# A planned TensorE order for the gate and pooling projections of a hybrid decoder block

## The chip, the cores and the metric

The kernel runs on one core of a Trainium2 chip, as one program. The metric is device time in microseconds (us); lower is better. Three runs of the kernel before gave 1358.35 to 1358.66, median 1358.63. A profiled execution of its own took 1358.44, and its trace is what is read below.

## The reference, cut to what matters

One layer of a decoder trunk steps 288 tokens (256 of a prompt, 8 samples of 4 tokens) of width 2048. All arrays are float32.

```
mod = silu(c) @ w_ada + b_ada                 # 9 conditionings x (6 parts x 2048)
h   = rmsnorm(x)*norm1 * (1 + sc1) + sh1      # parts 0, 1
u_pool, z, xbc, dt = split(h @ w_in)          # 512, 1536, 2560, 24 columns
pool_out = grouped causal means of u_pool, minus u_pool, @ pool_w[g] * pool_scale
xbc = silu(causal_conv4(xbc));  dt = softplus(dt + dt_bias)
y   = ssd_scan(xbc, dt) + D*x                 # 4 groups of 6 heads of 64, state 128
y   = rmsnorm(y * silu(z)) * ssd_norm
x   = x + g1 * (concat(pool_out, y) @ w_out)  # part 2
h2  = rmsnorm(x)*norm2 * (1 + sc2) + sh2      # parts 3, 4
x   = x + g2 * conv_ffn(h2)                   # part 5
```

## The kernel before, in words

Features lie on the partitions and tokens in the free dimension, so a projection is a series of matmuls with a 128x128 weight tile and 288 moving columns. For float32 accuracy each weight tile is split into a high and a low part of type fp32r (`split`, line 290: a ScalarE cast at line 286, a VectorE subtraction at line 288), the activations likewise, and each product is three fp32r matmuls (`mm3`, lines 300 to 302). All other TensorE work is plain float32: conditioning, transposes, the scan, the pooling maps, sums over partitions. One exception is `cse` (line 793), which is fp32r.

The stages follow one another: the first conditioning parts together with the `xbc` projections, the gate and pooling projections (`uz`, `uz_units`, line 885), the output projection (`out`), the up projections, and the down projections. This case is about `uz`: eight output tiles m = 10 to 15 (gates `z` of scan groups 2 and 3) and then m = 1 and 0 (pooling columns). `project_units` (line 306) yields every two k tiles, so one tile is 8 units of 6 matmuls, and the stage has 64 units.

Between units other generators are advanced by `pull`, each with a rate:

- `adas`: conditioning parts 2, 3 and 4 (`ada_part_units`, line 402). One visit loads four 512 KB pieces of `w_ada` and runs eight fp32 matmuls (16 rows in the trace, `adap`, line 329); the nine conditionings fill only 32 columns, so four of them lie beside each other in the array. Eight visits make a part; then come a copy (`asb`) and transposes with the bias (`adat`).
- `back`: the depthwise convolutions (`conv_group`, line 663), loads of the initial states (`h0s`), and the scan (`ssd_group`, line 714) of four groups. A scan group has transposes `xt` and `bt`, the products `cb`, state sums `s`, the old state's share `yo`, decays (`cse` on TensorE; Relu and Exp on ScalarE; products on VectorE) and, for each of three head pairs, the `y` products (lines 811 to 821), followed by line 823 and line 827 on VectorE and Square (line 829) on ScalarE.
- `y_norm` (line 896) sums the squares over partitions (`ysum`), takes sqrt on ScalarE and reciprocal on VectorE, spreads it with a matmul (`pbrstdy`) and scales the four `zy` tiles. `pool_units` (line 857) is the pooling.

The generators fix the program order only. Which instruction of an engine goes first is settled when the program is built, by the framework's scheduler, from its own estimate of when operands are ready and from priorities; on the chip each engine then runs its fixed order. `in_order` (line 208) adds dependences that hold the named engines to program order; before, it is used only at the very start.

Silu of z in groups 2 and 3 is taken straight from PSUM, tile by tile (line 893); groups 0 and 1 are taken three tiles at once (line 836). Eight raw weight buffers serve `uz` and `adap` loads in turn, all issued on SP (line 267); the state loads are issued there as well (line 702).

Of the kernel before, what the change touches and what calls it, by code (L numbers as in the profile page):

```python
# [12 lines left out]
F32 = mybir.dt.float32  # L13
# [5 lines left out]
P = 128  # L19
# [34 lines left out]
RA1, RA2, RB1, RB2, RB3 = 0.5, 0.4, 1.0, 1.0, 1.0  # L54
TA, ADA_OUT = 4, 4
TK = 4
# [105 lines left out]
def kernel(ctx: ExitStack, tc, ins, outs):  # L162
# [57 lines left out]

    wps = aux("warm")
# [104 lines left out]
    def ada_mm(ps, raw, k, c0, nb, js):  # L326
        for j in js:
            c = c0 + (j - js[0]) * nb
            nc.tensor.matmul(ps[32 * j:32 * j + 32, :nb], sc_c[:, k, :], raw[:, c:c + nb],  # L329
                             start=(k == 0), stop=(k == KT - 1), tile_position=(0, 32 * j))  # L330

# [331 lines left out]
    def conv_group(g):  # L663
# [5 lines left out]
        for r in range(5):  # L669
# [5 lines left out]
            for i in range(1, 4):  # L675
# [10 lines left out]
        nc.scalar.activation(cf[:, :, 0:NP], cf[:, :, 0:NP], AF.Silu)  # L686

        nc.scalar.activation(cf[:, :, NP:N].rearrange("p m (b l) -> p m b l", b=NB),
                             cf[:, :, 3 + NP:].rearrange("p m (b l) -> p m b l", l=7)[:, :, :, 0:NL], AF.Silu)
        yield  # L690
# [23 lines left out]
    def ssd_group(g):  # L714
# [12 lines left out]
        for c in range(3):  # L727
            pt = aux(f"xt{g}_{c}")
            for t in range(3):
                nc.tensor.transpose(pt[:, t * P:(t + 1) * P], toks(t, c), ident)  # L730
            nc.vector.tensor_tensor(heads(xdt[:, c, :]), heads(pt[:, :G6]), bc64(dt[:, c, hs]), ALU.mult)
            nc.vector.tensor_tensor(heads(xde[:, c, :]), heads(pt[:, :G6]), bc64(dtr["dtde"][:, c, hs]), ALU.mult)
# [13 lines left out]
        nc.vector.tensor_tensor(cb, pcb[:, :N], vec[:, K_TRI:K_TRI + N], ALU.mult)  # L746
# [3 lines left out]
        nc.gpsimd.dma_start(sbx[q, P:P + G6], xde[0:NS, 2, :])  # L750
        yield
# [20 lines left out]
        for i in range(2):  # L772
            for j in range(4):
# [5 lines left out]
        nc.vector.tensor_tensor(yo.rearrange("p (h q) -> p h q", h=HG),  # L779
                                py[:, :G6].rearrange("p (h q) -> p h q", h=HG),  # L780
                                bc64(dtr["ecs4"][:, hs]), ALU.mult)
        yield

        csr, cs = dtr["csr"], dtr["cs"]

        def decays(t):

            e = sx[0].tile([P, 2, N], F32, tag="e", name=f"e{g}_{t}", bufs=2)
# [630 lines left out]
```

## Time and profile before

| what | before |
|---|---|
| median of three runs | 1358.63 us |
| profiled execution, its own time | 1358.44 us |
| span of its trace | 1356.6 us |
| TensorE matmul busy | 1343.0 us |
| VectorE / ScalarE / GpSimd busy | 810.8 / 579.2 / 222.1 us |
| mean granted TensorE clock | 0.998 of 2.4 GHz |

The span is what the trace covers, from the first instruction to the last; 1.8 us of the execution lie around it. PE is TensorE, PEld its weight loads, DVE VectorE, ACT ScalarE, POOL GpSimd, SP SyncE. The record of a matmul is longer than its turn in the pipeline (matmuls of `uz` start 0.13 us apart and are recorded as 0.29 us), so starts are compared, not lengths. In the trace a plain float32 matmul leaves two rows. The page lists where the chain that ended last spent its time: 96% on PE.

### The profile page before, as it was taken

Reading aid. Unit: us, or ns where it says so; the run is one execution under the profiler, and the core shown is the slowest. Engines: PE = TensorE matmul, PEld = TensorE weight load, DVE = VectorE, ACT = ScalarE, POOL = GpSimd, SP = SyncE. Lnnn points to the kernel's source line nnn. Section 1 sums busy time; section 2 is a strip of 40 time slices with the busy share of each in tenths; the row PEclk is TensorE's granted clock in tenths of the full one; section 3 lists DMA queues with packets and bytes.
Section 4 is the critical chain, followed back from the end, with each engine's and each line's share of the span. In section 5 each row is a group of like instructions: output and inputs, shape, how many; then the busy total and the mean of one; then the engine's idle time right before and its main releaser. Section 6 shows DMA issues by size and latency. Waiting matters only on the chain.

```text
span 1356.6 us, 26243 instructions
## 1 busy us (share of the span) xinstructions
PE 1343.0 (99%) x10557; PEld 1247.6 (92%) x10557; DVE 810.8 (60%) x1349; ACT 579.2 (43%) x910; POOL 222.1 (16%) x433
## 2 busy tenths in 40 slices
PE   9999999999999999999999999999999999999997
PEld 8889988777779889999999999999999999999997
DVE  5675568678564448645565455656554556566553
ACT  5243234587643335534443334443433334434452
POOL 0000002123221213111221001312220012222221
PEclk9999999999999999999999999999999999999999
DMA  9999768877988877787555555555555555565531
GB/s 374 405 408 363 253 218 326 333 259 289 335 298 332 314 261 260 238 303 262 185 181 185 165 179 184 197 193 181 187 177 167 186 189 190 189 204 190 182 119 70
DMA packets 97481, 323.18 MB, mean 238 GB/s; under 512 B 10768, under 2 KB 19920, under 8 KB 97360
## 3 DMA queue, kind: packets, MB, share of 16 engines
q1 hardware_dynamic: 93600, 310.79, 64.6%
q0 software_dynamic: 3184, 9.69, 1.9%
q8 instruction: 82, 1.34, 0.4%
q10 hardware_dynamic: 576, 1.03, 0.2%
q14 instruction: 39, 0.32, 0.1%
HBM read 309.78 MB, written 10.39 MB: 236 GB/s over the span
## 4 chain that ended last, share of the span: by engine, by line
PE 96%; DVE 2%; DMA 1%; ACT 0%; issue 0%; SPq 0%; POOL 0%; DVEq 0%; POOLq 0%; ACTq 0%
PE mm_down L301 7%; PE mm_down L300 7%; PE mm_down L302 7%; PE mm_val L301 6%; PE mm_gate L301 6%; PE mm_gate L300 6%; PE mm_val L302 6%; PE mm_gate L302 6%; PE mm_val L300 6%; PE xbc L300 5%; PE adap L329 5%; PE xbc L301 4%; PE xbc L302 4%; PE mm_out L300 3%; PE mm_out L301 3%; PE mm_out L302 2%
## 5 line engine op out<-in xcount | busy, mean ns | idle before, releaser
L301 PE MATMUL mm_down<-al,whi_down 128*128 128x288 f32 x688 | 202.5, 294 | 0.0
L300 PE MATMUL mm_down<-ah,whi_down 128*128 128x288 f32 x688 | 202.4, 294 | 0.0
L302 PE MATMUL mm_down<-ah,wlo_down 128*128 128x288 f32 x688 | 202.0, 294 | 0.0
L301 PE MATMUL mm_gate<-h2l,whi_gate 128*128 128x288 f32 x640 | 188.8, 295 | 0.0
L301 PE MATMUL mm_val<-h2l,whi_val 128*128 128x288 f32 x640 | 188.8, 295 | 0.0
L302 PE MATMUL mm_val<-h2h,wlo_val 128*128 128x288 f32 x640 | 188.7, 295 | 0.0
L302 PE MATMUL mm_gate<-h2h,wlo_gate 128*128 128x288 f32 x640 | 188.6, 295 | 0.0
L300 PE MATMUL mm_gate<-h2h,whi_gate 128*128 128x288 f32 x640 | 188.5, 294 | 0.0
L300 PE MATMUL mm_val<-h2h,whi_val 128*128 128x288 f32 x640 | 187.7, 293 | 0.0
L288 DVE TENSOR_TENSOR wlo_gate<-raw_gate,whi_gate 128x1024 fp32r<-128x1024 f32 x80 | 97.9, 1226 | 136.4 <-ACT whi_gate L286 134.3
L288 DVE TENSOR_TENSOR wlo_down<-raw_down,whi_down 128x1024 fp32r<-128x1024 f32 x96 | 108.2, 1127 | 116.0 <-ACT whi_down L286 116.0
L286 ACT CAST whi_down<-raw_down 128x1024 fp32r<-128x1024 f32 x96 | 92.4, 962 | 167.3 <-PE mm_down L301 117.9
L286 ACT CAST whi_gate<-raw_gate 128x1024 fp32r<-128x1024 f32 x80 | 83.9, 1051 | 161.0 <-PE mm_gate L301 65.4
L286 ACT CAST whi_val<-raw_val 128x1024 fp32r<-128x1024 f32 x80 | 84.1, 1051 | 123.1 <-issue 98.6
L300 PE MATMUL xbc<-h1h,whi_xbc 128*128 128x288 f32 x448 | 133.5, 301 | 0.8 <-ACT h1h L450 0.7
L301 PE MATMUL xbc<-h1l,whi_xbc 128*128 128x288 f32 x448 | 132.0, 296 | 0.0
L302 PE MATMUL xbc<-h1h,wlo_xbc 128*128 128x288 f32 x448 | 130.1, 296 | 0.0
L300 PEld LDWEIGHTS mm_down<-ah,whi_down 128*128 128x128 f32 x688 | 129.2, 188 | 0.0
L301 PEld LDWEIGHTS mm_down<-al,whi_down 128*128 128x128 f32 x688 | 129.1, 188 | 0.0
L302 PEld LDWEIGHTS mm_down<-ah,wlo_down 128*128 128x128 f32 x688 | 129.0, 188 | 0.0
L300 PEld LDWEIGHTS mm_gate<-h2h,whi_gate 128*128 128x128 f32 x640 | 120.3, 188 | 5.0 <-ACT ah L1184 3.4
L300 PEld LDWEIGHTS mm_val<-h2h,whi_val 128*128 128x128 f32 x640 | 120.3, 188 | 0.0
(325 smaller groups left out, 2978.4 us busy)
## 6 DMA issues: line engine op xcount, KB each, us to landing
raw_adap<-wflat SPq DMA_DIRECT2D x128, 512.0 KB, 5.8
raw_gate<-wflat SPq DMA_DIRECT2D x80, 512.0 KB, 3.5
raw_val<-wflat SPq DMA_DIRECT2D x80, 512.0 KB, 3.7
raw_ada<-wflat SPq DMA_DIRECT2D x64, 512.0 KB, 9.7
raw_xbc<-wflat SPq DMA_DIRECT2D x50, 512.0 KB, 9.5
raw_down<-wflat SPq DMA_DIRECT2D x48, 512.0 KB, 3.5
raw_out<-wflat SPq DMA_DIRECT2D x32, 512.0 KB, 7.2
raw_down<-wflat SPq DMA_DIRECT2D x32, 384.0 KB, 3.0
```

The lines of the kernel that those rows point to most:

```text
L286: yield nc.scalar.copy(hi[:, :n], raw[:, a:a + n])
L288: yield hi, lo, nc.vector.tensor_tensor(lo[:, :n], raw[:, a:a + n], hi[:, :n].bitcast(F32), ALU.subtract)
L300: nc.tensor.matmul(ps, whi[:, w], bh, start=first, stop=False)
L301: nc.tensor.matmul(ps, whi[:, w], bl, start=False, stop=False)
L302: nc.tensor.matmul(ps, wlo[:, w], bh, start=False, stop=last)
L329: nc.tensor.matmul(ps[32 * j:32 * j + 32, :nb], sc_c[:, k, :], raw[:, c:c + nb], start=(k == 0), stop=(k == KT - 1), tile_position=(0, 32 ...
```

## The change

1. The `uz` stage is run under `in_order` for TensorE, and the rates are replaced by a plan: for each unit n from 0 to 64 a list of generators to advance once (`plan`, `at`, `step`). Scan group g starts at n = 15g - 6, its eight steps at the offsets `GS`; convolutions, state loads, conditioning visits (`VU`), pools (`PU`, `PL`) and the norm (`YN`) have unit numbers too. The `out` stage, from its second tile on, is also under `in_order`, and conditioning advances 5/7 step per tile there.
2. A conditioning visit asks for its pieces in order and uses them in the reverse order: its first matmul waits for the last piece, and the others are bound to follow it directly.
3. The scan group has eight steps instead of seven: the decays of a head pair come a step or more ahead of its `y`, with three buffers instead of two; the `y` products go column range by column range.
4. z of groups 2 and 3 is copied from PSUM and its Silu taken per group, after the last decays; Silu, Exp and Sqrt are held in program order on ScalarE (`tabled`), and a dummy Sqrt follows the last group.
5. Some VectorE operations of the scan get high priority.

```diff
+GA0, GP, GS = -6, 15, (0, 2, 3, 5, 6, 9, 12, 15)
+GCV, GH0 = (1, 3, 5, 7, 9, 11), 9
+VU = (6, 7, 9, 12, 18, 24, 33, 39, 48, 54, 61)
+YN = (58, 60)
+PU = (40, 42, 45, 46, 48, 51)
+PL = (58, 62)
...
     def ada_part_units(part, ay=1):
-        for k in range(KT):
-            raws = [load(("adap", part, k, h)) for h in range(2)]
-            for h in range(2):
-                ada_mm(ps, raws[h], k, 0, 512, range(2 * h, 2 * h + 2))
-            if k % ay == ay - 1:
-                yield
+        for ka in range(0, KT, ay):
+            raws = [(k, h, load(("adap", part, k, h))) for k in range(ka, ka + ay) for h in range(2)]
+            tied = False
+            for k, h, raw in raws[::-1]:
+                for j in (2 * h, 2 * h + 1):
+                    with tc.high_priority() if tied else nullcontext():
+                        i = nc.tensor.matmul(ps[32 * j:32 * j + 32, :512], sc_c[:, k, :],
...
+                    if tied:
+                        tc.keep_in_program_order(i)
+                    tied = True
+            yield
...
+        dec = [decays(0)]          # before s and yo; decays(1) after them
...
         dec.append(decays(1))
+        yield
+        dec.append(decays(2))
+        nc.scalar.activation(zy[g], zy[g], AF.Silu)
+        tabled()
         outputs(0, *dec[0])
         yield
-        dec.append(decays(2))
         outputs(1, *dec[1])
         yield
         outputs(2, *dec[2])
...
-            nc.scalar.activation(zy_of(g)[:, t, :], ps[:, :N], AF.Silu)
+            nc.scalar.copy(zy_of(g)[:, t, :], ps[:, :N])
...
+    for g in range(4):
+        if g:
+            for i in range(3 if g == 1 else 0, 6):
+                at(GA0 + GP * (g - 1) + GCV[i], convs[g])
+            at(GA0 + GP * (g - 1) + GH0, h0s(g))
+        for i in range(SSD0 if g == 0 else 0, 8):
+            at(GA0 + GP * g + GS[i], ssds[g])
+    for n in VU:
+        at(n, adas)
...
+    with in_order(nc.tensor.engine):
+        n = 0
+        step(0)
+        for m in list(range(4 + 3 * ZEARLY, 16)) + ULATE:
+            for _ in uz_units(m):
+                n += 1
+                if n % (KT // YK):
+                    step(n)
+            if m < 4:
+                next(late[m])
+            step(n)
+    pull(adas, TA)
...
-        for i, ps in enumerate(project_units(("out", m), KT, order=MIXK)):
-            if m == KT - 1 and i == 5:
-                all_but_last("ssum2")
+        with in_order(nc.tensor.engine) if m else nullcontext():
+            for i, ps in enumerate(project_units(("out", m), KT, order=MIXK)):
+                if m == KT - 1 and i == 5:
+                    all_but_last("ssum2")
+            pull(adas, ADA_OUT)
```

## Rows read from the trace of the kernel before

**Rows 1.** The page, busy time of each engine.

```profile
PE 1343.0 (99%) x10557; PEld 1247.6 (92%) x10557; DVE 810.8 (60%) x1349; ACT 579.2 (43%) x910; POOL 222.1 (16%) x433
```

**Rows 2.** Windows: stretch, its us, busy of PE, PEld, DVE, ACT, POOL; clock, DMA, GB/s.

```profile
700.00:800.00 100.00, 100.00 (x758) 100.00 (x757) 51.51 (x73) 35.42 (x42) 8.07 (x23) 1.00 0.52 173
198.00:258.00 60.00, 60.00 (x446) 46.40 (x444) 51.69 (x128) 25.60 (x36) 13.46 (x31) 1.00 0.86 322
260.00:338.50 78.50, 77.66 (x636) 55.75 (x632) 59.06 (x109) 62.08 (x138) 18.05 (x26) 1.00 0.78 288
338.50:374.80 36.30, 36.06 (x298) 27.64 (x296) 21.48 (x41) 22.22 (x50) 8.29 (x8) 1.00 0.89 326
374.80:390.40 15.60, 14.50 (x89) 8.64 (x89) 14.40 (x36) 8.45 (x18) 2.28 (x6) 1.00 0.86 306
```

**Rows 3.** Timeline of PE in `uz`: start us, length us, line, operation, rows.

```profile
325.39 1.93 PE L329 MATMUL adap<-raw_adap,sc_c 128*32 128x512 f32 x16
327.25 0.31 PE L811 MATMUL y<-vec,yo 128*64 128x32 f32 x4
...
328.52 0.29 PE L301 MATMUL mm_uz<-h1l,whi_uz 128*128 128x288 f32 x1
328.74 1.04 PE L329 MATMUL adap<-raw_adap,sc_c 128*32 128x512 f32 x2
329.72 0.40 PE L302 MATMUL mm_uz<-h1h,wlo_uz 128*128 128x288 f32 x1
329.96 0.30 PE L300 MATMUL mm_uz<-h1h,whi_uz 128*128 128x288 f32 x1
```

**Rows 4.** The same view, around a visit that a `y` interrupts.

```profile
265.18 1.90 PE L329 MATMUL adap<-raw_adap,sc_c 128*32 128x512 f32 x10
...
267.40 0.44 PE L820 MATMUL y<-e,xdt 128*64 128x128 f32 x4
267.62 0.44 PE L821 MATMUL y<-ec,s 128*64 128x128 f32 x4
267.99 1.06 PE L329 MATMUL adap<-raw_adap,sc_c 128*32 128x512 f32 x6
```

**Rows 5.** Chain that ended last, in order of time: start us, us, what.

```profile
201.80 0.97 PE adap L329 x2
...
263.72 0.27 PE y L811 x4
...
336.74 1.85 PE adap L329 x14
...
370.48 0.60 PE pbrstdy L251 x6
```

**Rows 6.** Timeline of PE at the start of `out`.

```profile
374.79 1.90 PE L329 MATMUL adap<-raw_adap,sc_c 128*32 128x512 f32 x10
...
388.72 1.06 PE L329 MATMUL adap<-raw_adap,sc_c 128*32 128x512 f32 x6
```

**Rows 7.** Timeline of PE and of ACT around the norm of y.

```profile
366.77 0.83 PE L238 MATMUL ysum<-ones,ssq 128*128 128x1 f32 x6 [0.24 <-POOL ssq L833]
...
370.32 0.75 PE L251 MATMUL pbrstdy<-early,r3rstdy 128*128 128x128 f32 x6
...
367.63 1.28 ACT L244 ACT_TABLE_LOAD   x1
```

**Rows 8.** ACT groups of 260 to 374.8: xcount, busy us, mean ns, idle before.

```profile
L799 ACT ACT_TABLE_LOAD x7 | 9.0, 1283 | 0.0
L893 ACT ACT_TABLE_LOAD x4 | 5.1, 1283 | 0.1
L686 ACT ACT_TABLE_LOAD x2 | 2.6, 1283 | 0.0
```

**Rows 9.** Waits of SP's queue in 260 to 374.8: us in total, times, longest us.

```profile
SPq L267 <- PE adap L329: 46.2, 10, 8.2
SPq L702 <- PE yo L775: 12.5, 2, 12.2
```

More of the change, by code (lines that the diff above doesn't have):

```diff
@@ new lines, in outputs @@
+        def outputs(t, e, ec):
+            assert (g, t) in zdone
+            pq = aux(f"y{g}_{t}")
+            rows = [slice(0, 64), slice(64, P)]
+            fs = [slice(64 * (2 * t + i), 64 * (2 * t + i) + 64) for i in range(2)]
+            prods = [(P, NP, lambda i: (s1[:, fs[i]], ec[:, i, :]), True, False),
+                     (P, NP, lambda i: (xdt[:, 1, fs[i]], e[:, i, P:NP]), False, True),
+                     (0, P, lambda i: (xdt[:, 0, fs[i]], e[:, i, 0:P]), True, True),
+                     (NP, N, lambda i: (xdt[:, 2, fs[i]], e[:, i, NP:N]), True, False),
+                     (NP, N, lambda i: (yo[:, fs[i]], seli), False, True)]
+            for n0, n1, ops, first, last in prods:
+                for i, r in enumerate(rows):
+                    nc.tensor.matmul(pq[r, n0:n1], *ops(i), start=first, stop=last)
+            yt = cf[:, t, 0:N]
+            with tc.high_priority():
+                nc.vector.scalar_tensor_tensor(out=yt, in0=yt,
+                                               scalar=vec[:, V_D + 3 * g + t:V_D + 3 * g + t + 1],
+                                               in1=pq[:, :N], op0=ALU.mult, op1=ALU.add)
+            zt = zy[g][:, t, :]
+            nc.vector.tensor_tensor(zt, zt, yt, ALU.mult)
+            sq = kp.tile([P, N], F32, tag="xsq", name=f"ysq{g}_{t}", bufs=2)
+            nc.scalar.activation(sq, zt, AF.Square)
+            if g + t == 0:
+                nc.gpsimd.tensor_copy(ssq, sq)
+            else:
+                nc.gpsimd.tensor_tensor(ssq, ssq, sq, ALU.add)
@@ L1028, with at, sqrt_ahead, step @@
                 pull(adas, RA1 / AY)
-    late = {}
-    n = 0
-    zlast = 3 * (4 - ZEARLY) * KT // YK
-    for m in list(range(4 + 3 * ZEARLY, 16)) + ULATE:
-        for _ in uz_units(m):
-            n += 1
-            for gn in late.values():
-                pull(gn, 0.5)
-            pull(adas, RA2 / AY)
-            pull(back, RB2 if n <= zlast else RB3)
-            if n == zlast:
-                drain(back)
-                back = chain(ssd3, y_norm())
-        if m < 4:
-            late[m] = pool_units(m)
-            next(late[m])
-    pull(adas, TA / AY)
+    drain(back)
+    yn = y_norm()
+    early_pool = chain(pool_units(UEARLY[0]), pool_units(UEARLY[1]))
+    late = {m: pool_units(m) for m in ULATE}
+    plan = [[] for _ in range(4 * KT + 1)]
+    def at(n, gn):
+        plan[max(n, 0)].append(gn)
+    for g in range(4):
[7 more added lines that the diff above has]
+        at(n, adas)
+    def sqrt_ahead():
+        nc.scalar.activation(warm, sc_c[:, 0, 0:1], AF.Sqrt, scale=0.0)
+        tabled()
+        yield
+    at(GA0 + 3 * GP + GS[-1], sqrt_ahead())
+    for gn, steps in ((early_pool, PU), (yn, YN), (late[ULATE[0]], PL)):
+        for n in steps:
+            at(n, gn)
+    def step(n):
+        for gn in plan[n]:
+            next(gn, None)
+    with in_order(nc.tensor.engine):
[10 more added lines that the diff above has]
+    pull(adas, TA)
     for h, (_, n) in enumerate(_halves(KT)):
@@ L1050 @@
         drain(gn)
-    drain(back)
+    drain(yn)
     npl = kp.tile([P, 4, 135], F32, tag="hmod", name="npl", bufs=2)
```

116 lines of the change are left out of this document (48 added, 68 removed).

## The prediction

> **What bounds the kernel now.** First the busy times of the page: PE 99% of the span [rows 1], and the chain that ended last lies on PE for 96%. So only what shortens PE's own work, or its few idle moments, can move the end. Then the windows, by stage. In a plain stretch (700 to 800) PE makes 758 matmuls in 100 us, one in 0.132 us [rows 2], and nothing else could be saved there. The change touches 198 to about 480. In `uz` (260.0 to 374.8) PE is idle for 0.84 + 0.24 = 1.1 us, in the 15.6 us after it for 1.1 us [rows 2]. Judged by idle time there is next to nothing to win.
>
> The timeline of PE says otherwise. Behind a piece of a visit (`adap` x2) the next `uz` matmul starts 0.98 us later, as if the visit's other fourteen rows had run too: a whole visit takes 327.25 - 325.39 = 1.86 us [rows 3]. The 2 + 14 rows of this broken visit take 0.98 + 1.85 [rows 3, 5], so the break costs 0.97 us. And every stretch of float32 work among the fp32r matmuls is paid for at its edges. The last fp32r matmul ahead of it keeps its place for 0.22 us (328.52 to 328.74), the first one behind it for 0.24 (329.72 to 329.96), both against 0.132: 0.09 + 0.11. The last rows of the stretch are slow too: the four of L821 hold 0.37 us, the four of L820, equal in shape, 0.22 [rows 4].
>
> The trace agrees here with the Trainium skill, page "Perfetto Trace Analysis", section "Identifying the Most-Contended Engine": matmul busy time does not tell how near PE is to its limit, weight-load busy time does. PEld is busy for all of 700 to 800 but for 83.4 of the 114.8 us of `uz` [rows 2]; by the page's rule up to 31 us are open there, by matmul busy time 1.1.
>
> **The change, part by part.** The sum is made against the profiled execution's 1358.44 us; the median of the runs lies 0.2 above it.
>
> *Fewer stretches.* The trace has 48 separate float32 stretches in `uz`, the first at 263.72, the last at 370.48 [rows 5]. The plan's lists give 23 unit numbers with float32 work on PE (n = 3, 6, 9, 11, 12, 14, 18, 21, 24, 26, 29, 33, 36, 39, 41, 44, 45, 48, 51, 54, 58, 61, 62), and `in_order` makes each one stretch, since whatever is due at one n is emitted together; `cse` is fp32r and needs no edge. A stretch costs 0.09 + 0.11 at its edges plus a tail between 0 and 0.15; I take 0.10, as L821 alternates with L820 and part of its 0.15 may be theirs. 25 x 0.30 = 7.5 us. About eleven of the merged ones put different shapes together (`y` before `adap`, `xt` or `pool`), and there the slow tail remains: L821 holds its 0.37 us ahead of `adap` at 267.99 too [rows 4]. 11 x 0.15 = 1.6 us goes back. Net 5.9 us, bounds 25 x 0.20 - 1.6 = 3.4 and 25 x 0.35 = 8.7.
>
> *Whole visits.* Four visits in `uz` are broken, the first at 265.18 (10 + 6 rows), the last at 328.74 [rows 3, 4]: 4 x 0.97 = 3.9 us. One in the `xbc` stage at 201.80 [rows 5] gives 0.97 and its second stretch 0.30. Together 5.2 us. The `xbc` stage has no planned order, only the binding inside a visit, so the lower bound is 3.9.
>
> *Into `out`.* The 15.6 us from 374.8 hold 48 matmuls of the first `out` tile (48 x 0.132 = 6.4), two visits in five pieces, the first at 374.79, the last at 388.72 [rows 6] (whole, and each with its stretch, 2 x 2.16 = 4.3), and two pooling maps and one set of transposes, for which I allow 1.7. That is 12.4, so 3.2 us go, 1.1 of them idle time. The visits themselves only move: both versions have nine in `uz` and eight behind it, and each costs its 2.16 wherever it stands.
>
> *Idle time in `uz`.* 1.1 us [rows 2] goes with the old order.
>
> *New waits.* PE may no longer fill a wait with other matmuls, and three places follow. (a) `ysum` and `pbrstdy` become neighbours, with sqrt and reciprocal between them. Before, 366.77 + 0.83 to 370.32 is 2.7 us, filled with `uz`; 1.28 of it was a table load [rows 7], which the dummy Sqrt at n = 54 now takes ahead. I take 1.4; bounds 0.5 and 2.7. The six units behind, the DVE instructions behind and all of `out` stand behind this wait. (b) The scan's operands from ACT and DVE. Up to n = 40 ACT was busy for 62.1 and DVE for 59.1 of 78.5 us [rows 2]; squeezed into some 69 us that is DVE 86%, and ACT, with about five of the loads of [rows 8] fewer up to there (6.4 us), about 81%. In 198 to 258 DVE was busy for 86% and PE lost nothing [rows 2], but there PE had other work to choose. The decays come two steps ahead of their `y`, so I take 2.0 us in all; bounds 0 and 9. (c) The first `out` tile needs `zy` scaled, cast and subtracted in turn. DVE was busy for 14.4 of the 15.6 us there [rows 2], and the norm comes at n = 58, with six units, a visit and a pool between it and `out`. I take 1.3; bounds 0 and 3.
>
> *Free.* Fewer table changes: seven loads ahead of Exp, four ahead of a tile's Silu, two ahead of the convolution's [rows 8] become about eight in all, and ACT is not on the chain; what hides them is PE's own work, and without that cover they would cost 1.28 us each. The new order of the `y` products keeps their number and widths (bounds -0.6 and +0.6). Third decay buffers and the priorities on DVE cost PE nothing. The out stage's order gains nothing, its visits being whole already.
>
> Sum: 5.9 + 5.2 + 3.2 + 1.1 = 15.4 off, 1.4 + 2.0 + 1.3 = 4.7 on. 1358.4 - 10.7 = **1347.7 us**.
>
> **The rivals.**
>
> *No new waits.* If (a) to (c) come to 1 us or less, the time is 1343.0 to 1344; with the upper bounds of the edges, 1340.2. For it: from 260 to 338.5 PE lost only 0.84 us beside an ACT that was busy for 62.1 of 78.5 us [rows 2]. Against it: (a) is certain to cost something.
>
> *DVE and ACT set the pace of `uz`.* With 86% and 81%, each in a fixed order, a late `cb`, `xdt` or cast stops PE. If the stretch up to n = 40 shrinks by 2.5 us only instead of 9.5, the time is 1354.7. For it: the close shares. Against it: 14% and 19% stay free, and each group's decays are ready ahead of use. The Trainium skill, page "ScalarE: Activation LUTs", section "What ACT_TABLE_LOAD costs", adds a drain of about 1380 ns to each load of 1283 ns. No row shows the drain, the idle time before the loads being 0.0 to 0.1 us [rows 8]. By the page's rule the five loads that remain up to n = 40 would bring ACT to about 92% of the squeezed stretch, and this rival would be the likeliest.
>
> *It does not matter.* If edges and broken visits are an artefact of modelled starts, PE was full with real work and the time stays at 1358.4. Against it: the starts are 0.98 us apart where only two rows of a visit run [rows 3].
>
> *Slower: visits wait for their last piece.* Before, a broken visit used what had landed and PE did other work until the rest came: 6 us at 201.80, 7 us between 329.72 and 336.74 [rows 3, 5]. Now the first matmul of a visit waits for the last piece, at a fixed place, and all of PE stands behind it. The place is SP's queue: its loads wait for raw buffers that the visit before frees, 46.2 us in ten waits, and once 12.2 us behind a state load whose buffer `yo` had not freed [rows 9]; the nine visits' loads and all `uz` weights queue behind such a wait. If three of nine visits wait 6 us each, 18 us are added: 1365.7. It decides from 10.7 / 9 = 1.2 us a visit. Against it: the DMA share of `uz` is 0.78 and 0.89 at 288 and 326 GB/s [rows 2]; 104 us in place of 114.8 ask for about 331 GB/s, and 198 to 258 had 322. Also the state loads are planned four units behind the `yo` that frees their buffers.
>
> **How the numbers follow.** A measurement tells about 0.2%, 2.7 us, from no change. Forecast, 1344 to 1351.5: 0.52. No new waits, 1340.2 to 1344: 0.15. DVE and ACT, 1351.5 to 1355.7: 0.15. No difference, within 2.7 us: 0.07. Slower: 0.11. So faster 0.82, same 0.07, slower 0.11. The range 1340.2 to 1356.0 leaves out the slower case and most of the no-difference case, 0.17 together.
>
> **What would show it.** Right: 23 or so float32 stretches in `uz`; every `adap` group of 16 rows in `uz` and `out`; `uz` taking 104 to 106 us; eight or nine table loads there; a bubble of about 1.4 us between `ysum` and `pbrstdy`; the first `out` tile done within 9 us of the last `uz` matmul. Wrong: PE waiting on DMA ahead of `adap` for more than 1 us a visit, PE waiting on DVE or ACT for more than 5 us in all, or a `uz` stage of about 115 us although stretches and broken visits are gone, which would disprove the price of the edges.

## The result, and the profile after

| what | before | after |
|---|---|---|
| median | 1358.66 us (15 runs, 1358.35 to 1359.94) | 1362.04 us (15 runs, 1359.80 to 1363.58) |
| ratio to before | | 1.0023, 95% interval 1.0016 to 1.0030 |
| profiled execution | 1358.44 us | 1362.68 us |
| span of its trace | 1356.6 us | 1360.9 us |
| mean granted TensorE clock of 2.4 GHz | 0.998 | 0.992 |

The change makes the kernel slower by 0.23%; 1347.7 us, faster, had been predicted. The spans differ by 4.3 us, and 3.4 of them lie in one part of the program. It begins with the 900th `xbc` matmul (at 168.64 us before, at 169.44 after; the 0.8 us between them are there at the first `xbc` matmul already, which starts between 18.0 and 18.9 us in the twenty profiles of this case) and ends with the first `mm_up`; what comes behind takes 850.4 and 850.5 us. The same work took 337.60 us before and takes 341.02 now. The windows of these two stretches (us of the stretch; busy time of PE, PEld, DVE, ACT, POOL; granted clock; DMA share; GB/s), before:

```profile
168.64:506.24 337.60, 335.42 (x2594) 267.31 (x2592) 213.55 (x418) 171.21 (x315) 67.96 (x111) 1.00 0.80 296
```

and after:

```profile
169.44:510.46 341.02, 329.67 (x2593) 269.39 (x2591) 217.16 (x419) 167.21 (x315) 72.01 (x111) 0.98 0.80 295
```

PE matmul busy time, 1343.0 us of the span in [rows 1], is 1336.8 now, in a longer span:

```profile
PE 1336.8 (98%) x10557; PEld 1249.2 (92%) x10557; DVE 813.6 (60%) x1349; ACT 573.1 (42%) x908; POOL 220.0 (16%) x433
```

PE was idle for 2.2 us of the stretch before (337.60 - 335.42) and is idle for 11.35 us now. And the granted clock is no longer 1.00. Narrow windows of after show where it stands at 0.50, that is at 1.2 GHz:

```profile
295.00:298.70 3.70, 1.59 (x10) 1.13 (x9) 3.15 (x5) 2.96 (x5) 1.18 (x1) 1.00 1.03 407
298.80:302.10 3.30, 3.30 (x27) 2.96 (x27) 2.37 (x5) 1.27 (x1) 0.20 (x1) 0.50 1.01 402
302.30:322.60 20.30, 18.21 (x149) 14.22 (x148) 13.39 (x22) 14.00 (x38) 3.21 (x7) 1.00 0.67 250
322.70:329.40 6.70, 5.17 (x36) 2.38 (x36) 6.44 (x12) 5.97 (x11) 2.66 (x3) 0.50 0.52 202
370.50:373.80 3.30, 3.30 (x16) 3.30 (x16) 2.08 (x5) 0.40 (x1) 1.71 (x1) 0.50 0.78 287
```

The three stretches are 3.41, 6.83 and 3.41 us long in the trace, 13.65 in all. The second begins while PE still waits, and 1.57 us of it are idle time already counted; PE works at half clock for the other 12.08 us, and half of that is lost: 6.0 us. So PE's own work, with idle time and lost clock taken off, went from 335.4 to 341.0 - 11.35 - 6.0 = 323.6 us. **The change took 11.8 us out of PE's work and put 9.2 us of waiting and 6.0 us of low clock in.** That is 3.4 us net, as much as the medians differ.

What PE waits for, over the whole span of after (us in all, times, longest):

```profile
PE y L818 <- ACT s L839: 3.7, 1, 3.7
PE mm_up L319 <- ACT h2h L471: 1.9, 1, 1.9
PE pbrstdy L270 <- DVE r3rstdy L264: 1.4, 1, 1.4
PE mm_uz L319 <- ACT whi_uz L305: 1.4, 1, 1.4
PE warm L245 <- DVE ones L200: 1.1, 1, 1.1
PE mm_out L320 <- DVE mixl L1127: 1.0, 1, 1.0
PE mm_uz L321 <- DVE wlo_uz L307: 0.9, 2, 0.7
```

Each of the three falls of the clock comes in or right behind one of the waits in `uz` and the norm: `whi_uz` and `wlo_uz` (up to 298.4), `s` (up to 324.2), `pbrstdy` (up to 370.3). The timeline of PE around the longest (start us, length us, line, operation, rows, idle time before), next to the same `y` and visit one group earlier:

```profile
291.05 0.44 PE L818 MATMUL y<-ec,s 128*64 128x128 f32 x4
...
292.06 1.92 PE L424 MATMUL adap<-raw_adap,sc_c 128*32 128x512 f32 x16
...
320.09 0.42 PE L791 MATMUL cse<-csr,selr 128*128 128x288 f32 x2
324.24 0.70 PE L818 MATMUL y<-ec,s 128*64 128x128 f32 x4 [3.72 <-ACT s L839]
...
326.09 3.59 PE L424 MATMUL adap<-raw_adap,sc_c 128*32 128x512 f32 x16
```

The visit is whole (16 rows, where [rows 3, 4] have 2, 10 and 6), but at half clock it takes 3.6 us in place of 1.9. The matmuls of the sums `s` end when those of `yo` begin, at 314.95. Their copy is a ScalarE instruction, and ACT's timeline shows what it stands behind:

```profile
314.32 1.04 ACT L305 CAST whi_uz<-raw_uz 128x1024 fp32r<-128x1024 f32 x1
315.25 0.81 ACT L796 ACTIVATE e<-cse,csd 128x128 f32<-128x128 f32 x3
...
321.72 0.82 ACT L796 ACTIVATE e<-cse,csd 128x128 f32<-128x128 f32 x3
...
323.16 0.65 ACT L694 ACTIVATE cf<-cvp,vec 128x312 f32<-128x312 f32 x1
323.70 0.48 ACT L839 COPY s<-s 128x384 f32<-128x384 f32 x1
```

Promoted decays, two casts and two convolution rows come first, without a gap. In the windows, ACT is busy for 4.73 us of the 12 before and for 14.53 of these 14.6:

```profile
300.00:312.00 12.00, 12.00 (x111) 10.13 (x108) 7.91 (x14) 4.73 (x7) 2.04 (x5) 0.91 0.68 254
312.00:326.60 14.60, 10.88 (x86) 8.32 (x88) 10.56 (x15) 14.53 (x39) 3.24 (x5) 0.87 0.73 279
```

### The profile page after: what moved, and what is told of

Same layout as the page of the kernel before. It is cut to its first block, busy times and chain, and to the rows that moved or that the text cites. A ratio compares the mean times of both kernels' runs of the same rounds, so it can differ in the third digit from the quotient of the medians.

```text
span 1360.9 us, 26223 instructions
## 1 busy us (share of the span) xinstructions
PE 1336.8 (98%) x10557; PEld 1249.2 (92%) x10557; DVE 813.6 (60%) x1349; ACT 573.1 (42%) x908; POOL 220.0 (16%) x433
## 4 chain that ended last, share of the span: by engine, by line
PE 93%; ACT 3%; DMA 2%; DVE 1%; issue 1%; SPq 0%; DVEq 0%; ACTq 0%
PE mm_down L320 7%; PE mm_down L319 7%; PE mm_down L321 7%; PE mm_val L320 6%; PE mm_gate L320 6%; PE mm_gate L319 6%; PE mm_val L321 6%; PE mm_gate L321 6%; PE mm_val L319 6%; PE xbc L319 4%; PE xbc L320 4%; PE xbc L321 4%; PE adap L424 4%; PE mm_out L319 2%; PE mm_out L321 2%; PE mm_out L320 2%
```

## The experiments

All kernels were read by the same ledger: the stretch from the 900th `xbc` matmul to the first `mm_up`, PE's idle time in it, the time lost to half clock (half of what PE worked at it), the time of unread matmuls, whose results nobody reads (0.132 us each), and what is left, PE's own work. The ledger is of the one profiled execution, the median and the ratio are of the timed runs, each against runs of before made beside it. Where the profiled execution is far from the median, as in e5 and h1 (2.0 and 1.4 us below) and in g2 and h2 (3.2 and 2.1 above), the row does not stand for a typical run.

| kernel | median us (runs) | profiled us | ratio to before, 95% | stretch | idle | lost clock | unread | own work |
|---|---|---|---|---|---|---|---|---|
| before | 1358.66 (15) | 1358.44 | | 337.6 | 2.2 | 0 | | 335.4 |
| after | 1362.04 (15) | 1362.68 | 1.0016 to 1.0030 | 341.0 | 11.4 | 6.0 | | 323.6 |
| e3 | 1358.18 (11) | 1357.38 | 0.9987 to 1.0004 | 335.8 | 6.8 | 1.7 | | 327.3 |
| e5 | 1360.77 (11) | 1358.79 | 1.0005 to 1.0023 | 337.8 | 7.0 | 2.9 | | 327.9 |
| e1 | 1364.64 (5) | 1365.11 | 1.0026 to 1.0051 | 344.0 | 14.9 | 5.5 | | 323.6 |
| e2 | 1363.87 (5) | 1363.87 | 1.0022 to 1.0048 | 342.0 | 10.9 | 7.8 | | 323.3 |
| f1 | 1359.51 (10) | 1359.92 | 0.9996 to 1.0016 | 338.1 | 6.0 | 0 | 7.7 | 324.5 |
| f2 | 1362.64 (10) | 1362.81 | 1.0017 to 1.0037 | 340.9 | 12.1 | 5.1 | | 323.7 |
| f3 | 1362.80 (6) | 1362.88 | 1.0017 to 1.0040 | 341.3 | 12.4 | 5.1 | | 323.8 |
| f4 | 1358.55 (10) | 1358.33 | 0.9992 to 1.0010 | 336.6 | 7.1 | 0 | | 329.5 |
| g1 | 1358.92 (11) | 1358.92 | 0.9995 to 1.0014 | 338.3 | 6.1 | 0 | 7.7 | 324.5 |
| g2 | 1359.26 (11) | 1362.43 | 0.9995 to 1.0013 | 340.9 | 12.8 | 3.4 | | 324.7 |
| g3 | 1358.21 (11) | 1358.21 | 0.9989 to 1.0007 | 336.4 | 9.1 | 1.7 | 1.5 | 324.1 |
| h1 | 1360.83 (10) | 1359.42 | 1.0006 to 1.0024 | 338.2 | 11.3 | 3.3 | | 323.5 |
| h2 | 1362.70 (6) | 1364.80 | 1.0015 to 1.0038 | 343.0 | 12.3 | 6.3 | | 324.4 |
| h3 | 1357.00 (11) | 1357.26 | 0.9978 to 0.9996 | 336.0 | 8.6 | 0 | 3.0 | 324.4 |
| h4 | 1357.47 (11) | 1357.47 | 0.9985 to 1.0002 | 336.6 | 4.0 | 0 | 9.2 | 323.4 |
| h5 | 1362.89 (10) | 1362.99 | 1.0018 to 1.0037 | 342.4 | 10.4 | 4.9 | 3.4 | 323.6 |
| h6 | 1365.11 (5) | 1365.11 | 1.0033 to 1.0058 | 343.4 | 14.4 | 5.1 | | 323.9 |
| h7 | 1356.28 (11) | 1355.89 | 0.9972 to 0.9990 | 335.1 | 4.0 | 0 | 3.0 | 328.1 |

**Are the gains at edges and visits real? e3** puts the new visits, and nothing else, into the kernel before:

```diff
-        for k in range(KT):
-            raws = [load(("adap", part, k, h)) for h in range(2)]
...
+        for ka in range(0, KT, ay):
+            raws = [(k, h, load(("adap", part, k, h))) for k in range(ka, ka + ay) for h in range(2)]
...
```

> The kernel before, with the visits made whole as in the change (first matmul waits for the last piece, the others bound behind it) and nothing else. Theory (a break in a visit costs 0.97 us): four broken visits in uz, one in xbc and one at the start of out become whole: 1358.7 - 6 x 0.97 = 1352.9, between 1352 and 1355 if some wait for their last piece. Rival (the price of a break is an artefact of modelled starts): 1358.7. Rival (visits that wait for the last DMA piece stop PE): over 1360.

Measured: 1358.18 us, no difference that can be told. But PE's own work fell by 8.1 us, and float32 stretches in this part from 79 to 72: 6 x 0.97 + 7 x 0.30 = 7.9, by the predicted prices. The theory's price holds and its time doesn't. The `uz` stage, with the same nine visits, takes 111.8 us (before: 114.6), which a price that is only an artefact of modelled starts could not bring about. PE came to the first `out` matmul at 373.7 (before: 379.5), and there it waited:

```profile
PE pool L889 <- DVE pout L884: 2.0, 2, 1.2
PE mm_out L301 <- DVE mixl L1076: 1.9, 1, 1.9
```

and fell to half clock for 3.4 us at 378.9. The rival that visits wait for DMA has nothing for it: no wait of PE on DMA is among e3's.

**e5** takes the strict TensorE order out of `uz`:

```diff
-    with in_order(nc.tensor.engine):
+    with nullcontext():
         n = 0
```

> The changed kernel, with uz's TensorE work free to be reordered by the scheduler (no in_order in uz); plan, decays ahead, Silu by group, priorities and whole visits stay. Theory (the strict order turns late ScalarE and VectorE results into waits of PE): PE fills the waits with other matmuls, its waits in uz fall from some 8 us to under 3, there is no half clock in uz, the float32 stretches are again over 22, each at about 0.3 us: 1350 to 1356. Rival (the waits come from ScalarE's order and load, whatever PE's order): 1360 to 1363.

The median is in the rival's range, yet in `uz` the waits went as the theory said: the idle time there is 1.7 us, with no half clock, and the first `out` matmul comes at 371.65 (after: 380.24). There PE waits 3.6 us for `mixl` and drops to half clock for 6.8 us. Own work is 327.9, near e3's, so about 4.3 us of the 11.8 are what the strict order adds (323.6). But the theory's reason is not shown by this. The scheduler arranged ScalarE anew as well, and the copy of `s` now follows its matmuls by 1.3 us where it was 8.7 in after:

```profile
313.89 0.49 ACT L839 COPY s<-s 128x384 f32<-128x384 f32 x1
```

`y` starts at 318.79, 4.4 us behind that copy's end. So here PE did not fill a wait for a late `s` with other work; `s` was no longer late.

**Does the clock fall because PE waits? f1** fills the three waits with matmuls that nobody reads, and changes nothing else:

```diff
+    def fill_pe(ps, n):
+        for _ in range(n):
+            nc.tensor.matmul(ps[:, :N], xhi[0][0][:, :P], xhi[0][0], start=True, stop=True)
...
         pb = aux("pb" + name)
+        fill_pe(pb, fill)
...
+        rstdyp, rstdy = rstd_of(psq, NH * 64, "rstdy", fill=11)
...
             pq = aux(f"y{g}_{t}")
+            fill_pe(pq, 28 if (g, t) == (2, 0) else 0)
...
+                if n == 20:
+                    fill_pe(aux("fill"), 19)
```

> The changed kernel, with 58 extra matmuls of 288 columns whose results nobody reads, put where PE waited: 19 ahead of the uz matmuls that wait for whi_uz and wlo_uz (from 295.5), 28 between the cse and the y that waits for s (320.3), 11 between ysum and pbrstdy (368.7). At 0.13 us each they take 2.5, 3.7 and 1.5 us, about as long as the waits, and nothing else moves. Theory (the granted clock falls because PE stands still there): the three stretches at half clock (13.65 us, in which 6.8 us are lost) are gone, the waits are filled and not shortened: 1362.0 - 6.8 = 1355.2, between 1354 and 1357. Rival (the clock falls for another reason, or at the next wait): half clock stays and the time is 1361 or more.

All three stretches at half clock are gone. Windows of f1:

```profile
260.00:507.00 247.00, 241.90 (x1963) 199.62 (x1962) 147.18 (x258) 128.19 (x254) 57.78 (x81) 1.00 0.82 301
507.50:510.70 3.20, 3.20 (x15) 3.20 (x15) 3.20 (x8) 0.00 (x0) 1.31 (x4) 0.50 1.04 411
```

So the wait is what lowers the clock. But the time fell by 2.5 us, not by the 6.8 expected. One fall now follows the second norm, outside the stretch. And at the `y` that waited for `s` the filling costs time. PE comes there 1.3 us earlier than in after (counted from the start of the stretch), and ACT's copy of `s` comes 1.3 us earlier too and ends at 322.38; but the unread matmuls first wait 1.4 us for ACT (`ec`), and then hold `y` back until 323.98, 1.6 us longer than `s` needs:

```profile
320.10 3.95 PE L262 MATMUL y<-h1h 128*128 128x288 f32 x28 [1.40 <-ACT ec L802]
```

```profile
321.90 0.48 ACT L845 COPY s<-s 128x384 f32<-128x384 f32 x1
```

f1's ten runs tell the same by themselves: at a mean clock of 0.998 or 0.997 they took 1357.23 to 1359.10, at 0.995 or 0.996 1359.92 to 1361.69.

**Where do the waits come from? e1** promotes the copy that stood behind the decays:

```diff
-        nc.scalar.copy(s1, ps1[:, :G6])
+        with tc.high_priority():
+            nc.scalar.copy(s1, ps1[:, :G6])
...
-        nc.scalar.copy(s2, ps2[:, :G6])
+        with tc.high_priority():
+            nc.scalar.copy(s2, ps2[:, :G6])
```

> The changed kernel, with the two ScalarE copies of the state sums (s1, s2) given the same high priority as the decays. Theory (the gains of the merged stretches are real and are given back where PE must wait for ScalarE, and by the lower granted clock that follows each wait): the copy no longer stands behind the promoted decays, the 3.7 us wait of y on s goes to under 0.5 us, and with it the 6.8 us at half clock from 322.7 (3.4 us of lost time). 1362.0 - 3.7 - 3.4 = about 1355, between 1354 and 1357. Rival (ScalarE's load sets the pace of the stage, whatever its order): the copy goes ahead, the decays come as much later, and PE waits for them instead: 1360 to 1363.

The wait on `s` is gone and a longer one has come, 13 us later; in PE's waits and ACT's timeline of e1:

```profile
PE xt L753 <- ACT cf L707: 6.7, 1, 6.7
```

```profile
323.91 2.32 ACT L694 ACTIVATE cf<-cvp,vec 128x312 f32<-128x312 f32 x4
...
328.65 0.63 ACT L694 ACTIVATE cf<-cvp,vec 128x312 f32<-128x312 f32 x1
...
336.37 1.27 ACT L707 ACTIVATE cf<-cf 128x1280 f32<-128x1280 f32 x1
```

The convolution of the next group, whose last row begins at 328.65, ends on VectorE so late that its Silu starts at 336.37, and `xt` and all of PE wait for it. The theory that one copy stands wrongly falls; the rival is right that the time comes back, though not through the decays, and the time lies above its range.

**f2** promotes the convolutions too, on both engines:

```diff
+            with tc.high_priority() if g else nullcontext():
                 nc.scalar.activation(o, cvp[g][:, r, 0:CV], AF.Identity,
...
```

> The changed kernel with the copies of s1 and s2 promoted (as in e1) and the convolutions of groups 1 to 3 promoted too, on ScalarE and VectorE. Theory (in e1 the wait moved to the convolution, whose steps stood behind promoted work on ScalarE and VectorE): the 6.7 us wait of xt on cf goes to under 1 us and with it one or both of the stretches at half clock: 1355 to 1359. Rival (ScalarE and VectorE have too little time for a group in 15 units whatever their order): the same amount of waiting, some 8 us or more in uz, turns up elsewhere (casts, decays, xdt): 1361 to 1366.

The 6.7 us are gone, and the waits are spread over the decays (`ec`, 1.4 twice), `yo` (1.1), a visit's DMA (2.3) and others: 12.1 us in all. It comes out as the rival said, by time and by waiting. **g2** instead moves the decays' ScalarE part to where ACT was idle:

```diff
+        dec = [decays(0)]
         for c in range(3):
             pt = aux(f"xt{g}_{c}")
...
+        dec.append(decays(1))
         bt = sx[0].tile([P, 3, P], F32, tag="bt", name=f"bt{g}")
...
-        dec.append(decays(1))
-        yield
+        times_cb(*dec[1])
         dec.append(decays(2))
+        yield
+        times_cb(*dec[2])
```

> The changed kernel, with the ScalarE part of the decays (cse, Relu, Exp) of a group moved ahead: those of the first head pair to the group's first step, of the second to its second step, of the third to the step where the second's stood; the products with cb stay where y needs them. In the trace of the changed kernel ScalarE is busy for 4.7 of the 12 us from 300 and for 14.5 of the 14.6 us from 312. Theory (the late s, cast and convolution are a matter of when ScalarE's work comes, not of how much there is): the idle time takes the decays, the 3.7 us wait of y on s goes to under 1 us, no stretch of half clock stands at 322, PE waits in uz for under 3 us in all: 1352 to 1357. Rival (ScalarE and VectorE have too little time for a group in 15 units): waits of 6 us or more in uz stay, wherever they are: 1360 to 1364.

The wait on `s` is gone with its half clock, and 2.8 us of the median, which lies between the two ranges. But `xt` now waits for `ec`, `xde` and `cf`, 4.6 us in all, half clock follows the last of these waits (at 334.4), and `mm_up` waits 2.6 us for `h2h`: idle time 12.8 us, 7.4 of it in `uz`, as the rival had it. **g3** adds the 11 unread matmuls of f1 at the norm and takes the urgency from two splits of the up projections.

> g2 with 11 unread matmuls between ysum and pbrstdy, as in f1, and the splits of the up projections' third and fourth tile not urgent, as in f3. Theory: the half clock at 370 goes (1.7 us) and the wait at the second norm shrinks by 1.2: 3 us less than g2. Rival (what is gained before 370 is given back there, since the first out tile waits for the scan's last results): g2's time within 1 us.

It is 1.05 us below g2: the rival, near enough. The half clock behind the norm (368.5 in g2) went, and one came at 379, where the first `out` tile waits 1.7 us, and one at 505.8, behind the second norm. **e2**, which had put `uz` matmuls between `ysum` and `pbrstdy` by giving the norm three unit numbers and as many steps, shows the same from the other side.

```diff
-YN = (58, 60)
+YN = (58, 60, 61)
```

> The changed kernel, with the norm of y spread over three unit numbers: column sums, sqrt and reciprocal at n = 58, the spreading matmul pbrstdy at 60, the first scaling at 61, so that uz matmuls stand between ysum and pbrstdy. Theory (each wait of PE costs itself and the half clock behind it): the 1.4 us wait goes and the 3.4 us at half clock from 370.45 with it (1.7 us lost): 1362.0 - 3.1 = about 1359, between 1358 and 1360; the half clock at 298.8 and 322.7 stays. Rival (the clock falls for another reason, at this place or a later one): the wait goes but half clock stays somewhere in 366 to 380: 1360.6. Rival (the first out tile then waits for zy, scaled later, as much longer): 1362.

The 1.4 us wait went, and `mixl`, scaled later, made the first `out` tile wait 2.9 us and the clock fall there for 6.8 us: the last rival, and 1.9 us worse than it said.

**Is it the amount of ScalarE's or VectorE's work?** h1 and h2 leave some of it out. In h2 ScalarE and VectorE keep nearly the order they have in after; in h1 the scheduler arranged both anew, so h1 changes the order along with the amount.

```diff
-                for c in range(3):
-                    n = slice(c * P, min(c * P + P, N))
-                    nc.scalar.activation(e[:, i, n], pe[:, n], AF.Relu, bias=cs[:, c, hh:hh + 1], scale=-1.0)
+                nc.scalar.activation(e[:, i, :], pe[:, :N], AF.Exp)
```

> The changed kernel with less work for ScalarE, in its order: the Relus of the decays and the Exp behind them are left out, one Exp per head straight from the cse takes their place (the output is then not the layer's). It takes some 1.5 us from each of the twelve decays, 18 us from ScalarE in all. Theory now (in uz a group's chain through ScalarE and VectorE has hardly any slack in 15 units, so whatever PE gains ahead it waits for later): with the chain shorter the waits of y on s and of uz on its cast go, the half clock with them, and the time comes to the forecast: 1347 to 1352. Rival (fixed order alone: s stands behind the same instructions): the 3.7 us wait shrinks by 2 to 3 us only, half clock stays at one or two places: 1355 to 1358. Rival (it is VectorE): 1360 to 1362.

ACT's busy time in the stretch fell from 167.2 to 151.7 us, and the wait on `s` went, but the time only by 1.2 us, into the range of the rival "it is VectorE". The subtraction of a split is late now: its cast ends at 293.91, and it starts at 295.80, behind other VectorE work. In PE's waits of h1:

```profile
PE mm_uz L321 <- DVE wlo_uz L307: 4.1, 2, 3.0
```

Half clock follows for 6.8 us (297.5). **h2** leaves out two of three taps of the convolutions (`range(1, 2 if g else 4)`):

> The changed kernel with less work for VectorE, in its order: two of the three multiply-add taps of each convolution row in groups 1 to 3 are left out (the output is then not the layer's): 30 instructions of some 0.5 us. Theory (VectorE holds the chain as much as ScalarE does): waits in uz shrink by 3 us or more and a stretch of half clock goes: 1354 to 1358. Rival (ScalarE alone holds it, as y's wait on s says): 1361 to 1363.

VectorE has 14.7 us less to do (202.5 for 217.2), and every wait of after stands where it stood: 3.7 on `s`, 1.4, 1.4, 1.0. So it isn't VectorE's amount of work. For ScalarE's amount h1 leaves the question open, since its order moved too; the forecast's time came with neither. What all these kernels have in common is a fixed order on three engines, tied to a fixed order on PE.

**The first `out` tile and the second norm. f3** issues one more visit ahead of `out` (`TA` 3 for 2) and makes two splits of the up projections' weights not urgent (`urgent=k > 3`); **f4** is the same without the strict order in `uz`.

> The changed kernel with two places eased. One more conditioning visit is issued ahead of the first out tile, where PE waits 1.0 us for mixl; and the splits of the third and fourth tile of the up projections' first weights are no longer urgent, so that they don't run ahead of the chain from the second norm (rstd, h_n, h2h). Theory: from the last uz matmul to the second out tile PE does 2 us more work in the same time (the visit is hidden), and the wait of mm_up on h2h falls from 1.9 to about 0.7: 1362.0 - 1.0 - 1.2 = 1359.8, between 1358.5 and 1361. Rival (the first out tile is bound by VectorE, which the visit's loads and splits delay further; the second norm's chain is late for another reason): 1361.5 or more.

> The changed kernel without the strict TensorE order in uz (as in e5) and with the two easings of f3. Theory (each is a place of its own, and the half clock at 376 in e5 follows the 3.6 us of waiting in the first out tile): the visit fills 2 of these 3.6 us, the half clock there goes (3.4 us), and the second norm gives 1 us: e5's 1360.8 - 2 - 3.4 - 1 = about 1354.5, between 1353 and 1357. Rival (the waits move on, as in e1): 1359 to 1361.

In both the visit is hidden (the first `out` tile is done at about 389 and 384 us, with one visit more done by then than in after and e5, which reach that point at about 389 and 385), and the wait of `mm_up` falls to 0.5 and 0.6 us, as the theory had it. But PE pays for it later: two waits of 1.3 us for the split (cast and subtraction) of `out` weights, which after has not. f3's time is its rival's; f4's half clock is gone, its time between theory and rival. **g1**, f1 with the two splits not urgent, shows that the second edit does nothing by itself:

> f1 (unread matmuls in the three waits) with the splits of the up projections' third and fourth tile not urgent. Theory: the wait of mm_up for h2h, 1.9 us in f1, falls to about 0.7, and the half clock at 507 that followed it (1.7 us) goes: 1359.5 - 2.9 = about 1356.6, between 1355.5 and 1358. Rival (the half clock stays there or moves): 1358 to 1359.5.

`mm_up` still waits 1.8 us for `h2h`, and the time is the rival's. So what shortened that wait in f3 and f4 is the moved visit, or both edits together; the runs don't tell. What makes the second norm late is in ACT's timeline of after:

```profile
506.20 0.83 ACT L305 CAST whi_upk<-raw_upk 128x768 fp32r<-128x768 f32 x1 [1.13 <-DMA raw_upk<-wflat]
506.94 0.39 ACT L277 COPY rstd<-pbrstd 128x288 f32<-128x288 f32 x1
509.25 0.83 ACT L305 CAST whi_upk<-raw_upk 128x768 fp32r<-128x768 f32 x1 [1.91 <-DMA raw_upk<-wflat]
509.99 0.76 ACT L471 CAST h2h<-h_n 128x288 fp32r<-128x288 f32 x2
```

The casts of the next `upk` weights stand ahead of the copy of `rstd` and of `h2h`, and ACT waits for their DMA first. **h4**, f1 with one more visit ahead of the up projections (`GA = (2, 4)`) and 12 unread matmuls ahead of the first `out` tile, undoes that: the copy of `rstd` and two `h2h` casts come first again, as before, and PE waits 0.5 us there, for a piece's DMA. (In the code the extra visit's load is issued ahead of those weights' loads; why the casts came first in after isn't shown.)

> f1 (the changed kernel with unread matmuls in its three waits) with 12 unread matmuls ahead of the first out tile and one more conditioning visit ahead of the up projections. Theory: the 1.9 us wait for h2h is filled with the visit, and the half clock that followed it in f1's profile goes: 1359.5 - 1.9 - 1.7 = about 1356, between 1354.5 and 1357.5. Rival (the visit delays the chain of the second norm as long as it lasts): 1358 to 1360.

1357.47, 2.0 us below f1, no half clock; theory's range. **h3** has the same two additions on g2 (the first decays behind `xt`) with g3's norm:

> A version to beat both: the changed kernel with the decays' ScalarE part early as in g2, but the first pair's behind the xt transposes; 11 unread matmuls between ysum and pbrstdy; 12 more ahead of the first out tile, where g3 waited 1.7 us and fell to half clock; and one more conditioning visit of part 5 ahead of the up projections, where PE waits 1.3 to 2.6 us for h2h. Theory (each wait filled with work that is to be done anyway, or kept from lowering the clock): g3's 1358.2 less 1.7 for the clock at 379, 1.7 for the clock at 506 and 1.3 for the visit: 1353 to 1356. Rival (the waits move on again): 1357 to 1359.

1357.00: the low edge of the rival's range, 1 us above the theory's, and the first version whose whole interval lies below 1.

**Visits in the waits. h5** lets work that is to be done anyway take the place of most unread matmuls; **h6** drops the rest of them.

```diff
-VU = (6, 7, 9, 12, 18, 24, 33, 39, 48, 54, 61)
+VU = (6, 7, 9, 12, 20, 24, 39, 48, 54)
...
         tabled()
+        if g == 2:
+            next(adas)
         outputs(0, *dec[0])
...
-        rstdyp, rstdy = rstd_of(psq, NH * 64, "rstdy")
+        rstdyp, rstdy = rstd_of(psq, NH * 64, "rstdy", mid=lambda: next(adas))
```

> The changed kernel with its waits filled by work that is to be done anyway. Three visits get another place in the plan: that of n = 18 to n = 20, ahead of the half tile whose cast is late (in place of f1's 19 unread matmuls); that of n = 33 from behind y to between cse and the y that waits for s; that of n = 61 to between ysum and pbrstdy. One visit of part 5 more ahead of the up projections, as in h4. Unread matmuls only for what a visit (1.86 us) leaves: 14 ahead of the same y, 12 ahead of the first out tile. Theory (what ends these waits is settled by ScalarE's and VectorE's order, so work of PE moved into them is free): h4's 1357.5 less 44 x 0.132 = 5.8 us of unread matmuls that the visits replace, less up to 1 us where a wait moves: 1351.5 to 1354. Rival (the moved visits push the chain back through cse and their own loads): 1356 to 1359.

> h5 without any unread matmul. Theory: the wait of y on s keeps about 1.9 to 3 us and the first out tile 1 to 1.7; half clock follows the first, perhaps both (1.7 us each): 1 to 4 us above h5, with more scatter from run to run. Rival (what is left of the waits is too short to lower the clock): h5's time or up to 0.5 us less.

h5 is on its rival's side, and worse than that had it; h6, 2.2 us above h5, is in its own theory's range. In h5 the visit does fill the wait on `s`. But behind `y` it had covered the next group's convolution, and PE's waits of h5 now have

```profile
PE xt L757 <- ACT cf L711: 3.3, 1, 3.3
PE mm_out L324 <- DVE mixl L1135: 2.1, 1, 2.1
```

with 6.8 us of half clock behind the first and 3.4 behind the second. h6 has 4 us more of idle time: `y` waits 1.9 us for `s` again, this time without a fall of the clock, the first `out` tile 3.3.

**h7** keeps the strict order only where no scan work is left, in the last `uz` tile and in `out`, with 11 and 12 unread matmuls and `GA = (2, 4)`:

```diff
-    with in_order(nc.tensor.engine):
...
+        with in_order(nc.tensor.engine) if m == ULATE[-1] else nullcontext():
...
+            if m == ULATE[-1]:
+                fill_pe(aux("fillo"), 12)
```

> The changed kernel with the strict TensorE order in the last uz tile and in out alone: in the seven uz tiles with scan work the scheduler orders PE (as in e5). In the strict part 11 unread matmuls between ysum and pbrstdy and 12 ahead of the first out tile; one more visit of part 5 ahead of the up projections. Theory (the waits in uz come from tying PE's order to ScalarE's and VectorE's own fixed orders, so that a late result of either stops all of PE; where PE may go on with uz matmuls they vanish): PE's waits in uz come to under 2.5 us, no half clock anywhere, the edges cost some 3 us more than in h3: e5's 1360.8 less 3.4 of half clock, 2 at the first out tile and 1.2 at the second norm: 1353 to 1356. Rival (the first out tile is bound by the scan's last results, so that PE's lead is lost there whatever fills it): 1356 to 1358, as h3 and h4.

1356.28 us, ratio 0.9981 (0.9972 to 0.9990), faster than both kernels and the lowest of all; the median lies 0.3 above the theory's range, at the low edge of the rival's. The numbers are as the theory has them: 1.7 us of idle time in `uz`, the clock at 1.00 in the whole stretch, own work 3.7 us above h3's. Its reason is no better shown than in e5: ScalarE's order is e5's again, with the copy of `s` at 314.65, 1.3 us behind its matmuls. Window and waits of h7:

```profile
168.70:503.83 335.13, 331.11 (x2617) 269.45 (x2615) 214.51 (x418) 166.71 (x313) 72.75 (x111) 1.00 0.81 299
```

```profile
PE pool L917 <- DVE pout L912: 1.6, 2, 0.8
PE warm L245 <- DVE ones L200: 1.1, 1, 1.1
```

## Why the prediction was wrong

**Fewer stretches, whole visits, into `out`: right.** Their sum, without the idle time in them, was 5.9 + 5.2 + 3.2 - 1.1 = 13.2 us; PE's own work fell by 11.8, and the float32 stretches of this part from 79 to 54. In `uz` there are 23, as forecast, and nine visits of 16 rows. The stage took 114.6 us before and takes 117.6 (first to last `mm_uz`), which the prediction had named as a sign against the price of the edges; but 7.5 us of waiting and 6.0 of lost clock are in it, and what is left, 104.1 us, is what the sum's own terms give ahead of its waits: 114.8 - 5.9 - 3.9 - 1.1 = 103.9. (With the 3.4 us of (a) and (b) they give 107.3, not the 104 to 106 that the prediction names as its sign.) e3 showed the two prices apart from the rest.

**Free: right, with one step missed.** `uz` and its norm now have eight table loads, where "about eight in all" were predicted against thirteen [rows 8]:

```profile
L870 ACT ACT_TABLE_LOAD x4 | 5.1, 1283 | 0.1
L797 ACT ACT_TABLE_LOAD x3 | 3.8, 1283 | 0.0
L1081 ACT ACT_TABLE_LOAD x1 | 1.3, 1283 | 0.0
```

The idle time before them is 0.0 to 0.1 us again, so the drain of the Trainium skill's page "ScalarE: Activation LUTs", section "What ACT_TABLE_LOAD costs", is not seen here either. Missed was that another program order of the loads and visits can change the order on ACT as far as the second norm: "The out stage's order gains nothing" was true, but 1.9 us of waiting at `mm_up` stand behind it.

**New waits: (a) and (c) right, (b) mis-sized.** (a) `pbrstdy` waits 1.41 us for 1.4 predicted; (c) the first `out` tile 1.05 for 1.3. (b) was taken as 2.0 us with bounds 0 and 9, "the decays come two steps ahead of their `y`". The decays did come early. They were promoted past everything, and so it was `s`, a cast and its subtraction that came late: 3.72 + 1.38 + 0.73 + 0.2 = 6.0 us. The prediction looked at the share of time that ACT and DVE are busy, and that did not decide it: with 15 us less of either (h1, h2) nothing like the forecast came about, while e1, with the same work and the copies of `s` promoted, lost the wait on `s` and got another. It is the order of an engine that must be read, behind which instruction each operand of PE's next stands.

**Not in the sum at all: the granted clock.** It costs 6.0 us. Before, it stayed at 1.00 in all five windows of [rows 2], although PE had idle moments there. The prediction priced a wait at its own length; each of the three places in `uz` and its norm cost most of its length again, or more (1.7 us for 2.1 of waiting, 2.6 for 3.7, 1.7 for 1.4); f1, which filled them, had no fall there. With (b) and the second norm's wait at their measured size the sum would have been 1347.7 + 4.0 + 1.9 = 1353.6, still faster; 0.8 us of waiting in `xbc` (0.3 to 0.8 in the same place of the other changed kernels, 0.05 in e5 and h1) and the clock bring it to 1360.4. The 1.4 us that PE's work fell short and the 0.8 ahead of the stretch make it 1362.6, and the profiled execution took 1362.68.

**The rivals.** The slower one named the wrong mechanism: no visit waits for its last piece (after's list of PE's waits has none on DMA), though SP waits for buffers nearly as long as in [rows 9]:

```profile
SPq L286 <- PE adap L424: 34.5, 9, 7.5
SPq L286 <- DVE wlo_uz L307: 21.3, 7, 4.8
```

"DVE and ACT set the pace" came nearest, with the right engines and the wrong reason, their busy share. "It does not matter" is refuted by the ledger. Of what was to show the forecast wrong, "PE waiting on DVE or ACT for more than 5 us in all" came true.

What stays open: what (b) would be if ScalarE and VectorE were planned by hand as PE is, or if PE were strict over the ScalarE order of e5 and h7. Neither was tried; every kernel here left their order to the scheduler, and it changed with PE's. So that the waits came with the strict order is shown (e5, h7); whether by PE's order or by the one that ScalarE got with it is not.

## What to carry to other kernels

A strict order on one engine is safe only as far as the engines that feed it are ordered with it. Where their orders come from the scheduler, look in the new trace where each operand's instruction now stands, and let the scheduler arrange all the engines together where it did better (here `uz`, but for its last tile: h7). Price a wait of TensorE in a full stretch at between one and about two times its length, and look at the granted clock of each stretch, not at the mean of the span. When a wait goes and the time does not, look for the next wait on the same chain before looking for another cause.

## What the runs showed of the hardware that was not expected

The granted clock went to half after waits of 1.4 us (`pbrstdy`) and of 1.4 + 0.7 (`whi_uz`, `wlo_uz`) in a stage that is otherwise full, and stayed there for 3.4 or 6.8 us. The same wait did not always do it: the 1.4 us at `pbrstdy` lowered the clock in the profiles of after, f2, g2 and h2 and not in those of e1, f3 and h1, and the 1.9 us at the second norm did in f1's and not in after's. It fits this that runs of one kernel scatter more where PE waits (after: 3.8 us from lowest to highest, before: 1.6). The Trainium skill, page "TensorE: Matmul & The Clock Gate", section "HAM oscillation — how this bites in real kernels", tells of a kernel whose TensorE goes back to the low clock in every wait for data; the traces here agree that a wait can do it, after 1.4 us as told above, and differ in that not every wait does. Matmuls whose results nobody reads can keep the clock up: 58 of them, 7.7 us, removed 6.0 us of loss from the stretch (f1).
